# Two B blocks of column pair 1 kept in DRAM in 16 bits, and a new last pair for the row groups of a matmul in Strassen-Winograd form

## The chip, the cores and the metric

The kernel runs on one core of a Trainium2 chip. The metric is the device time of one execution in microseconds (us); a time "before" is the median of three runs of the kernel without the change. The engines are TensorE (PE; weight loads are listed apart as PEld), VectorE (DVE), ScalarE (ACT), GpSimd (POOL) and SyncE (SP). SP, ACT and POOL also issue DMAs, each through a queue of its own, and each issues in program order.

## The reference

```python
# a, b: float32, 4096 x 4096; alpha = 0.01
x = np.matmul(a, b)
return np.where(x > 0, x, alpha * x)
```

The output is float32. The kernel multiplies in 16 bits. It also measures the operands while it runs (row sums of squares of A, sums of squares of B) and has a branch at the end that does the work again in another 16-bit format where the measures ask for it; with this input the branch isn't taken.

## The kernel before, in words

**Tiles.** The output is cut into 4 row groups of 1024 rows (index g) and 4 column pairs of 1024 columns (index j). One (g, j) is a *region*. In a region, A's 1024 rows and B's 1024 columns are each halved in both directions: a11, a12, a21, a22 (512 rows by 2048 of the contraction) and b11, b12, b21, b22 (2048 by 512 columns). Each block is held as two units of 1024 in the contraction (k = 0, 1); a unit is 1 MB in 16 bits. Region (0, 0) is computed plainly while the first data arrive (lines 286 to 483). All others use seven block products instead of eight (line 636), in the order a11, a12, s2, s3, s1, a22, s4, where s1 to s4 are sums of A blocks and B's partners are sums too. They are made on VectorE, A's by `sum_a` (549, the work at 541) once for a row group, B's by `b_sum` (569, 571) in place in every region. In the regions of groups 1 to 3 that don't turn (see below; the code's `in_quarters`), products 5 and 6, and product 3 too except in a group's first region, are cut into quarter products (735).

**A region's course** (the loop from 766). A product (785) sums 64 matmuls into four banks, y or z, by turns. Product 0 goes to y, which ScalarE copies out (`keep`, 798); product 1 to z, which VectorE adds to it (`add`, 942); VectorE applies the leaky function (309) and SP stores the result (948). Product 2 goes on top of y and ScalarE copies y again; product 3 opens z, copied by ScalarE; product 4 goes on top of y, and VectorE adds y to product 3's copy; product 5 goes on top of z, which VectorE adds; product 6 goes on top of y, and ScalarE copies it. So a product that goes on top of banks waits for the copy or addition that reads them.

**Order of the regions** (490). Group 0: pairs 1, 2, 3. Groups 1 and 3: pairs 2, 0, 1, 3. Group 2: 2, 0, 3, 1. A group's last region is *turning* (771): beside its own products it brings in the next group's A, except in group 3. A comes in 16 pieces (`pieces_a`, four each for a11, a12, a21, a22): POOL fetches a piece in four DMAs that turn float32 into 16 bits (131) into one of three a16 buffers, VectorE transposes it (140), and ScalarE squares and sums its rows (590). A buffer is free for the next piece when both are done. `bring_a` (973) does the three steps in this order; `fetch_a` and `square_a` do one. `note_rows` (592, 596) adds the row sums to the measure.

**B's way in.** `fetch_unit` (504) brings one unit of the next region's B. Pair 2 (`CACHED`) is written to DRAM in 16 bits in group 0 and comes back from there by SP (512). All other units come from the float32 input by POOL, two DMAs each, which turn them into 16 bits on the way (515). `fetch_b` is called four times in a region: for b12 after product 3, for b11 after product 4, for b21 before product 6, for b22 after it. The tiles of a block have two buffers, so a fetch waits until the present region's unit has been used for the last time.

**B's measure.** `Measure` (214) squares a block's four parts on ScalarE (229) and sums and folds them on VectorE (238 to 262). `EARLY` (627) lists the blocks measured at a region's start, `MEASURED` (630) those at other places, `IN_ROOM` (634) the block measured in a turning region, in the room of the tile that the next group's s2 will take. Each block of each pair is measured once.

**Nothing is scheduled by a tool.** Every engine does its instructions in the order of the code. What a line comes after in the code, on its engine, is what it waits behind. The lines that the change touches are 490 (order), 504 to 519 (`fetch_unit`), 627 to 634 (where blocks are measured), 1036 to 1071 (between products 1 and 3) and 1091 to 1132 (between product 3 and product 5).

Of the kernel before, what the change touches and what calls it, by code (L numbers as in the profile page):

```python
# [8 lines left out]
P = 128  # L9
DT = mybir.dt.float16  # L10
# [14 lines left out]
KC = 8  # L25
# [5 lines left out]
NT = 512  # L31
MT = 4
RM = MT * P

TURNS = [[0], [0, 1], [1, 2, 3], [2, 3]]
CACHED = 2

# [7 lines left out]
def kernel(  # L47
# [17 lines left out]
    nc = tc.nc  # L65
# [4 lines left out]
    G = M // (2 * RM)  # L70
# [8 lines left out]
    dram_pool = ctx.enter_context(tc.tile_pool(name="kept", bufs=1, space=bass.MemoryType.DRAM))  # L79
# [16 lines left out]
    half = per * P // 2  # L96
# [77 lines left out]
    def rows_of(mat, u, c, wide, whole):  # L174

        if u >= 2 or whole:
            per = 2 * KC
            k0 = u // 2 * 2 * KW
            c += u % 2 * KC
        else:  # L180
            per = KC // RUNS[u]
            k0 = u * KW + c // per * per * P
        return mat[k0:k0 + per * P, :].rearrange("(p c) n -> p c n", p=P)[:, c % per:c % per + wide, :]
# [153 lines left out]
    for what, i, *more in order:  # L337
        if what == "a":
            r, tiles = more
            k = slice(r * rw, (r + 1) * rw)  # L340
# [106 lines left out]
    for i in range(1, len(steps)):  # L447
        t, h, u, first, last = steps[i]
# [16 lines left out]
        t, h, u, first, last = steps[i]  # L465
# [20 lines left out]
    kept = dram_pool.tile([2, KU * KW, NT], DT, name="kept")  # L486

    kept_t = {name: dram_pool.tile([2, P, KC * NT], DT, name=f"kept_{name}") for name in ("t3", "t2")}
    regions = [(0, j) for j in range(1, J)]
    regions += [(g, j) for g in range(1, G) for j in ([2, 0, 3, 1] if g == 2 else [2, 0, 1, 3])]  # L490

    def fetch_b(i, quads, ks):

# [10 lines left out]
    def fetch_unit(i, u, nt):  # L504
        g, j = regions[i]
        half = u // 2
        t = b_pool.tile([P, KC, NT], DT, name="b", tag=f"b{half + 1}{nt + 1}")
        have_b[i, u, nt] = t
        if g > 1 and j == CACHED and (half, nt) == (0, 1):
            move_t("t3", t, u, False)  # L510
        elif g and j == CACHED:
            nc.sync.dma_start(t, rows_of(kept[nt], u, 0, KC, True))
        else:
            for c in range(0, KC, 4):
                nc.gpsimd.dma_start(t[:, c:c + 4, :], b_rows(j, u, c, 4, nt, g > 0))  # L515
            if j == CACHED:
                wide = KC // (RUNS + [1, 1])[u]
                for c in range(0, KC, wide):
                    nc.sync.dma_start(rows_of(kept[nt], u, c, wide, False), t[:, c:c + wide, :])
# [29 lines left out]
    def sum_a(g, name):  # L549
        blk = lambda h, half, k: at[g, h, 2 * half + k]  # L550
        if name != "s3" and (g, name, 0) not in s:
            new_s(g, name)
        for k in range(2):
            if name == "s1":
                a_sum(s[g, "s1", k], blk(1, 0, k), blk(1, 1, k), ADD)
            elif name == "s2":
                a_sum(s[g, "s2", k], s[g, "s1", k], blk(0, 0, k), SUB)
            elif name == "s3":
                s[g, "s3", k] = blk(1, 0, k)
                a_sum(s[g, "s3", k], blk(0, 0, k), blk(1, 0, k), SUB)  # L560
            else:
                a_sum(s[g, "s4", k], blk(0, 1, k), s[g, "s2", k], SUB)
# [29 lines left out]
    def note_rows(but=0):  # L592
        while len(rows_made) > but:
            r = rows_made.pop(0)
            for n, op in enumerate((MAX, MIN, ADD)):
                nc.vector.tensor_tensor(stats[:, n, 0], stats[:, n, 0], r, op)

    def judge(line):
# [26 lines left out]
    A11, A12, A22 = (0, 0, 0), (0, 0, 1), (0, 1, 1)  # L625
    B11, B12, B21, B22 = ((1, half, nt) for half in range(2) for nt in range(2))
    EARLY = {
        (1, 0): [B11], (1, 1): [B11, B21], (2, 0): [B12, B21], (2, 3): [B11], (3, 1): [B12], (3, 3): [B21],
    }
    MEASURED = {  # L630
        (0, 1): (None, [A11], B12, B11), (0, 2): (B21, [B22, A22], B12, A12),
        (3, 0): (B22, [], None, None),
    }
    IN_ROOM = {(1, 3): B22, (2, 1): B22}

    PRODUCTS = [("a11", 0, 0), ("a12", 1, 0), ("s2", 0, 0), ("s3", 0, 1), ("s1", 0, 0), ("a22", 1, 0), ("s4", 1, 1)]

# [14 lines left out]
    def b_quarter(t):  # L652
        return t.rearrange("p (c n) -> p c n", n=HALF)

    def quarters_of_b(i, half, nt):
        return {(k, n): have_b[i, 2 * half + k, nt][:, :, n * HALF:(n + 1) * HALF]
                for k in range(2) for n in range(2)}
# [8 lines left out]
    def sums_of_b(y, to, some=(2, 4, 1)):  # L666
        tt = nc.vector.tensor_tensor
        f = lambda n: b_quarter(to[n])
        if 2 in some:
            tt(f(2), y[0, 1], y[0, 0], ADD)  # L670
        if 4 in some:
            tt(f(4), y[1, 0], f(2), SUB)
        if 1 in some:
            tt(f(1), y[1, 1], f(2), SUB)  # L674
# [27 lines left out]
    def load_x21(g, name):  # L702

        if g:
            for c in range(KC // 2):
                nc.sync.dma_start(by_chunk(x21(g, name))[:, c], by_chunk(kept_x21[name])[:, c])

    def sums_of_s3(g, some, room=None):

        x = {key: by_chunk(q) for key, q in quarters_of_a(g, "s3").items()}  # L710
        rooms = s3_rooms(g)
        sx = {n: by_chunk(room) for n, room in rooms.items()}
        for n in some:
            if n == 4:
                sx[4] = by_chunk(room)
            x0, x1, op = {1: (x[1, 0], x[1, 1], ADD), 2: (sx[1], x[0, 0], SUB),
                          3: (x[0, 0], x[1, 0], SUB), 4: (x[0, 1], sx[2], SUB)}[n]
            nc.vector.tensor_tensor(sx[n], x0, x1, op)  # L718
            if n == 4:
                nc.sync.dma_start(kept_s3, room)  # L720
# [45 lines left out]
    for i, (g, j) in enumerate(regions):  # L766

        ks = (1, 0) if in_quarters else (0, 1)
# [3 lines left out]
        B = lambda half, nt, k: have_b[i, 2 * half + k, nt]  # L772
# [184 lines left out]
        coming = {}  # L957
# [5 lines left out]
        def fetch_a(h, half, n):  # L963
            if n == 0:
                coming["rows", h, half] = small_pool.tile([P, 16], FP32, name="rows", tag=f"rows{half}")
            coming[h, half][n][0]()

        def square_a(h, half, n):
            square_rows(coming[h, half][n][1].held[0], n, coming["rows", h, half])
            if n == MT - 1:  # L970
                rows_made.append(coming["rows", h, half])

        def bring_a(h, half, some=range(MT)):
            if turning:
                for n in some:
                    fetch_a(h, half, n)
                    coming[h, half][n][1]()
                    square_a(h, half, n)
# [19 lines left out]
        for n, m in enumerate(early):  # L998
            if n:
                m.begin()  # L1000
            m.end()
        have_t2 = g > 1 and j == CACHED
        if have_t2:
            for k in ks:
                t = have_b[i, k, 0] = b_pool.tile([P, KC, NT], DT, name="b", tag="b11")
# [4 lines left out]
        for k in ks:  # L1010
# [5 lines left out]
            b_sum(B(0, 0, k), B(0, 1, k), B(0, 0, k), ADD)  # L1016
            if g == 1 and j == CACHED:
                move_t("t3", B(0, 1, k), k, True)
# [17 lines left out]
        if in_fourth:  # L1036
            tq = {n: new_a16() for n in (2, 4)}
            sx4 = new_a16()
            if not second_of_group:
                nc.sync.dma_start(sx4, kept_s3)  # L1040
            t3_of_b(quarters_of_b(i, 0, 1))
            sums_of_b(quarters_of_b(i, 0, 1), tq, (2, 4))
            if second_of_group:
                sums_of_s3(g, (4,), sx4)
        for k in ks:
            b_sum(B(1, 0, k), B(1, 0, k), B(0, 0, k), SUB)
        if first_of_group and g:
# [10 lines left out]
        if in_quarters:  # L1058
            t = x_pool.tile([P, 4, QUARTER], DT, name="q", tag="x")
# [3 lines left out]
        for k in ks:  # L1063
            b_sum(B(0, 0, k), B(1, 1, k), B(0, 0, k), SUB)
        if g:
            bring_a(0, 1)
        note_rows(1)
        if i == 0:
            sum_a(g, "s4")
        if late_ones:  # L1070
            late_ones[0].end()
        if in_quarters and first_of_group:
# [14 lines left out]
        if in_quarters:  # L1087
            tq = {2: t[:, 0], 1: t[:, 1], 4: t[:, 2]}
        fetch_b(i + 1, [(0, 1)], (1, 0) if in_fourth else ks)
        in_room = None  # L1090
        if turning:
            room = new_s(g + 1, "s2").rearrange("p k c m e -> p (k c m e)").bitcast(BF16)
            if (g, j) in IN_ROOM:
                in_room = measure(i, *IN_ROOM[g, j], room.rearrange("p (n w) -> p n w", n=4))
                in_room.begin()
            bring_a(1, 0, [0])
            if in_room:
                in_room.end()
            bring_a(1, 0, [1])
            for n in (2, 3):  # L1100
                fetch_a(1, 0, n)
            load_x21(g, "a22")
            load_x21(g, "s4")
        for m in late_ones[1:]:
# [18 lines left out]
        if in_quarters:  # L1123
            tq, sq = sixth_in_quarters(u2_pairs, [new_bank(zbank + mt) for mt in range(MT)], v_pairs, v, y, tq, sq)
# [1 line left out]
            add(v, y)  # L1126
            leave(v_pairs, 1, 1)
        if turning:
            for n in (2, 3):
                coming[1, 0][n][1]()  # L1130
                square_a(1, 0, n)
            note_rows(1)
# [48 lines left out]
    with inputs.Else():  # L1181
        for m in range(M // RM):
            a_blocks = []
            for u in range(KU):
                t = a_pool.tile([P, KC // 2, RM, 2], BF16, name="a", tag=f"a{u // 2 + 1}{m % 2 + 1}")
# [6 lines left out]
            for n in range(N // NT):  # L1192
                banks = [new_bank(n % 2 * 4 + mt) for mt in range(MT)]
                cols = slice(n * NT, (n + 1) * NT)
                for u in range(KU):
                    t = b_pool.tile([P, KC, NT], BF16, name="b", tag=f"b{u // 2 + 1}{n % 2 + 1}")
# [8 lines left out]
                for mt in range(MT):  # L1205
                    t = c_pool.tile([P, 2, NT], FP32, name="c", tag=f"c{side}")[:, 0]
# [38 lines left out]
```

## Time and profile before

| what | before |
|---|---|
| runs | 1562.06, 1563.91, 1565.93 us; median 1563.91 |
| profiled execution, its own time | 1564.15 us |
| its span, first to last instruction | 1562.4 us |
| mean granted TensorE clock | 0.995 |
| busy: VectorE, ScalarE, POOL | 1138.7, 424.3, 300.4 us |
| TensorE's waits, whole list | 16.1 us |
| DMA | 339.71 MB, mean 217 GB/s |

Some regions in the same execution:

| region | from, to (us) | length | VectorE busy | ScalarE busy | DMA share |
|---|---|---|---|---|---|
| (0,1) | 122.56 to 219.26 | 96.70 | 77.17 | 28.66 | 0.89 |
| (0,3), turning | 315.95 to 412.64 | 96.69 | 61.67 | 49.03 | 0.97 |
| (1,2), after a turn | 412.64 to 506.16 | 93.52 | 84.43 | 13.91 | 0.92 |
| (1,3), turning | 690.03 to 794.77 | 104.74 | 68.20 | 51.57 | 0.95 |
| (2,2), after a turn | 794.77 to 890.28 | 95.51 | 78.24 | 17.84 | 0.96 |
| (2,1), turning | 1074.26 to 1180.96 | 106.70 | 68.21 | 51.57 | 0.94 |

How to read the views: a row of the timeline gives start and length in us, engine, line, operation, tiles, shapes and count, and in square brackets how long the engine stood idle before it and what ended that. A row of the waits gives who waited for whom, the total in us, how often, and the longest. A row of windows gives the stretch, its length, the busy time of PE, PEld, DVE, ACT and POOL with their counts, the granted clock of TensorE (1.00 is full speed), the DMA share and GB/s. A row of the queues gives packets, MB, and the time of the packets as a share of 16 DMA engines' span. An idle engine matters only where TensorE waits for it.

### The profile page before, as it was taken

Reading aid. Unit: us, or ns where it says so; the run is one execution under the profiler, and the core shown is the slowest. Engines: PE = TensorE matmul, PEld = TensorE weight load, DVE = VectorE, ACT = ScalarE, POOL = GpSimd, SP = SyncE. Lnnn points to the kernel's source line nnn. Section 1 sums busy time; section 2 is a strip of 40 time slices with the busy share of each in tenths; the row PEclk is TensorE's granted clock in tenths of the full one; section 3 lists DMA queues with packets and bytes.
Section 4 is the critical chain, followed back from the end, with each engine's and each line's share of the span. In section 5 each row is a group of like instructions: output and inputs, shape, how many; then the busy total and the mean of one; then the engine's idle time right before and its main releaser. Section 6 shows DMA issues by size and latency. Waiting matters only on the chain. (4 is left out here: it accounts for less than half of the span.)

```text
span 1562.4 us, 21610 instructions
## 1 busy us (share of the span) xinstructions
PE 1535.1 (98%) x8571; PEld 838.1 (54%) x8571; DVE 1138.7 (73%) x1179; ACT 424.3 (27%) x730; POOL 300.4 (19%) x482
## 2 busy tenths in 40 slices
PE   9999999999999999999899999999989999999997
PEld 4444444444447475574344757566434475746656
DVE  4378758766697787857569897674956967777686
ACT  2201224646300214105631130211553103021310
POOL 5641110243102020123310202012331110201100
PEclk9999999999999999999999999999999999999999
DMA  9999794998889899699698969979979895998933
GB/s 246 185 216 188 153 280 145 186 186 183 244 311 284 197 207 250 170 270 224 140 283 274 294 167 253 220 171 277 212 150 296 239 281 141 260 221 163 272 119 138
DMA packets 217729, 339.71 MB, mean 217 GB/s; under 512 B 19089, under 2 KB 162705, under 8 KB 209682
## 3 DMA queue, kind: packets, MB, share of 16 engines
q0 software_dynamic: 149376, 141.59, 56.7%
q1 hardware_dynamic: 61618, 171.08, 30.2%
q10 hardware_dynamic: 6624, 25.56, 4.3%
q8 instruction: 69, 1.13, 0.3%
q14 instruction: 42, 0.34, 0.1%
HBM read 374.34 MB, written 103.29 MB: 306 GB/s over the span
## 5 line engine op out<-in xcount | busy, mean ns | idle before, releaser
L785 PE MATMUL ps<-b,a 128*128 128x512 f16 x2752 | 600.8, 379 | 6.3 <-ACT c L798 4.6
L785 PE MATMUL ps<-b,s 128*128 128x512 f16 x2240 | 494.3, 381 | 7.4 <-DVE c L942 7.3
L785 PEld LDWEIGHTS <-a 128*128 128x128 f16 x2752 | 269.0, 98 | 332.1 <-issue 10.4
L785 PEld LDWEIGHTS <-s 128*128 128x128 f16 x2240 | 220.1, 98 | 274.9 <-issue 15.3
L515 POOL DMA_DIRECT2D b<-in_b_dram x184 | 136.6, 747 | 902.5 <-PE ps L735 348.1
L571 DVE TENSOR_TENSOR b<-b 128x4096 f16<-128x4096 f16 x104 | 235.1, 2288 | 80.9 <-DMA b<-in_b_dram 71.6
L798 ACT COPY c<-ps 128x512 f32<-128x512 f32 x172 | 88.6, 596 | 448.2 <-PE ps L785 397.5
L140 DVE STREAM_TRANSPOSE a<-a 128x512 uint32<-128x512 uint32 (+2 forms) x120 | 127.0, 1105 | 106.5 <-DMA a<-in_a_dram 106.5
L131 POOL DMA_DIRECT2D a<-in_a_dram x252 | 137.8, 552 | 234.9 <-ACT junk L590 82.7
L590 ACT ACTIVATE junk<-a 128x512 bf16<-128x512 f16 x192 | 121.1, 631 | 138.4 <-DMA a<-in_a_dram 113.4
L735 PEld LDWEIGHTS <-q 128*128 128x128 f16 x1392 | 136.1, 98 | 16.3 <-DVE q L718 0.6
L309 DVE SCALAR_TENSOR_TENSOR c<-c 128x1024 f32<-128x1024 f32 (+1 forms) x121 | 141.4, 1209 | 4.4 <-ACT c L798 4.2
L942 DVE TENSOR_TENSOR c<-ps,c 128x512 f32<-128x512 f32 x142 | 88.8, 683 | 49.2 <-PE ps L785 32.7
L229 ACT ACTIVATE sq<-b 128x2048 bf16<-128x2048 f16 x56 | 104.4, 1910 | 59.9 <-DVE sq L238 42.4
L281 PE MATMUL ps<-b,a 128*128 128x512 f16 x512 | 112.7, 379 | 2.0 <-DMA b<-in_b_dram 0.9
L735 PEld LDWEIGHTS <-a 128*128 128x128 f16 x1040 | 101.7, 98 | 15.8 <-DVE q L674 0.4
L735 PE MATMUL ps<-b,q 128*128 128x256 f16 x752 | 88.1, 273 | 0.3 <-DVE q L718 0.3
L281 PEld LDWEIGHTS <-a 128*128 128x128 f16 x512 | 49.7, 98 | 62.8 <-issue 3.9
L883 ACT COPY c<-ps 128x512 f32<-128x512 f32 x9 | 5.3, 586 | 268.7 <-PE ps L735 179.0
L735 PE MATMUL ps<-b,a 128*128 128x256 f16 x656 | 77.2, 273 | 0.0
L836 DVE TENSOR_TENSOR c<-ps,c 128x512 f32<-128x512 f32 x80 | 52.3, 685 | 14.8 <-PE ps L735 14.8
L735 PEld LDWEIGHTS <-s 128*128 128x128 f16 x592 | 57.9, 98 | 6.7
(112 smaller groups left out, 880.5 us busy)
## 6 DMA issues: line engine op xcount, KB each, us to landing
b<-in_b_dram POOLq DMA_DIRECT2D x192, 512.0 KB, 15.0
out_dram<-c SPq DMA_DIRECT2D x240, 256.0 KB, 6.1
a<-in_a_dram POOLq DMA_DIRECT2D x244, 128.0 KB, 5.7
b<-kept SPq DMA_DIRECT2D x20, 1024.0 KB, 9.9
q<-kept_qs ACTq DMA_DIRECT2D x40, 512.0 KB, 7.8
s<-kept_s SPq DMA_DIRECT2D x18, 1024.0 KB, 7.3
q<-kept_qa SPq DMA_DIRECT2D x28, 512.0 KB, 7.3
b<-in_b_dram POOLq DMA_DIRECT2D x24, 256.0 KB, 9.1
```

Of the source, the lines that this page charges most:

```text
L131: nc.gpsimd.dma_start(a16[32 * q:32 * q + 32], src.rearrange("(g i) w -> i g w", i=32))
L140: nc.vector.transpose(part.rearrange("p c m e -> p c (m e)").bitcast(U32) .rearrange("p c (g i) -> p g c i", i=32), src[:, :, i * n:(i + 1 ...
L229: nc.scalar.activation(to, self.parts[n], SQUARE)
L281: nc.tensor.matmul(ps, a_cols(at[0, h, u], c, mt, (h, u) == (0, 0)), bt[0, u, nt][:, c, :], start=first, stop=last,)
L309: nc.vector.scalar_tensor_tensor(t, t, alpha, t, op0=MULT, op1=MAX if alpha <= 1 else MIN)
L515: nc.gpsimd.dma_start(t[:, c:c + 4, :], b_rows(j, u, c, 4, nt, g > 0))
L571: nc.vector.tensor_tensor(f(to), f(x0), f(x1), op)
L590: nc.scalar.activation(junk, piece[:, q, :], SQUARE, accum_out=to[:, 4 * n + q:4 * n + q + 1])
L735: nc.tensor.matmul(to[m], xq[:, c // 2, rows, c % 2], yq[:, c, :], start=first and c == 0 and m < banks, stop=c == KC - 1, skip_group_chec ...
L785: nc.tensor.matmul(banks[mt], a_cols(t, c, mt, t is first_a), B(half, nt, k)[:, c, :], start=first and (k, c) == todo[0], stop=(k, c) == t ...
L798: nc.scalar.copy(kept[mt], banks[mt])
L942: nc.vector.tensor_add(to, bank, to)
```

## The change

`kept_last` is a new DRAM tensor. In region (0,1) the four units of b21 and b22 are stored there by SP in 16 bits, after product 1's outputs, before b21 is overwritten by its sum; groups 1 to 3 load these units of pair 1 from there by SP, and no longer from the input by POOL. s4's sum of group 0 moves ahead of b21's sums in (0,1). The order of groups 1 and 2 becomes 2, 0, 3, 1, so that regions (0,3), (1,1) and (2,1) turn. b22's measure in a turning region is now made in (0,3) and (1,1), directly after product 3's copies and at one go; (2,1) has none of this kind. `EARLY` is rearranged to match. In a turn of groups 1 and 2, a12's last piece comes after product 3's copies and that measure; in every turn, of a21's pieces only the first is transposed and squared ahead of product 4's addition, and the other three after it (before: two and two). s3's fourth sum of a group's second region in quarters moves between two B sums.

Counted in the built program: TensorE has the same instructions in the same order; SP gains 4 stores and 12 loads; POOL loses 24 loads of half a unit; VectorE and ScalarE have as many instructions as before.

```diff
 CACHED = 2
+LAST = 1
...
     kept_t = {name: dram_pool.tile([2, P, KC * NT], DT, name=f"kept_{name}") for name in ("t3", "t2")}
+    kept_last = dram_pool.tile([2, 2, P, KC * NT], DT, name="kept_last")
     regions = [(0, j) for j in range(1, J)]
-    regions += [(g, j) for g in range(1, G) for j in ([2, 0, 3, 1] if g == 2 else [2, 0, 1, 3])]
+    regions += [(g, j) for g in range(1, G) for j in ([2, 0, 3, 1] if g < G - 1 else [2, 0, 1, 3])]
...
             nc.sync.dma_start(t, rows_of(kept[nt], u, 0, KC, True))
+        elif g and j == LAST and half:
+            nc.sync.dma_start(t.rearrange("p c n -> p (c n)"), kept_last[u - 2, nt])
         else:
...
     EARLY = {
-        (1, 0): [B11], (1, 1): [B11, B21], (2, 0): [B12, B21], (2, 3): [B11], (3, 1): [B12], (3, 3): [B21],
+        (1, 0): [B11], (1, 3): [B11], (2, 0): [B12, B21], (2, 3): [B21], (2, 1): [B12], (3, 1): [B11, B21],
     }
...
-    IN_ROOM = {(1, 3): B22, (2, 1): B22}
+    IN_ROOM = {(0, 3): B22, (1, 1): B22}
...
-            sums_of_b(quarters_of_b(i, 0, 1), tq, (2, 4))
+            sums_of_b(quarters_of_b(i, 0, 1), tq, (2,))
             if second_of_group:
                 sums_of_s3(g, (4,), sx4)
+            sums_of_b(quarters_of_b(i, 0, 1), tq, (4,))
+        if (g, j) == (0, LAST):
+            for nt in range(2):
+                for k in ks:
+                    nc.sync.dma_start(kept_last[k, nt], B(1, nt, k).rearrange("p c n -> p (c n)"))
+        if i == 0:
+            sum_a(g, "s4")
         for k in ks:
             b_sum(B(1, 0, k), B(1, 0, k), B(0, 0, k), SUB)
...
         if g:
-            bring_a(0, 1)
-        note_rows(1)
-        if i == 0:
-            sum_a(g, "s4")
+            bring_a(0, 1, range(3))
...
                 in_room.begin()
-            bring_a(1, 0, [0])
-            if in_room:
                 in_room.end()
-            bring_a(1, 0, [1])
-            for n in (2, 3):
+            if g:
+                bring_a(0, 1, [3])
+            note_rows(1)
+            for n in range(3):
                 fetch_a(1, 0, n)
+            coming[1, 0][0][1]()
+            square_a(1, 0, 0)
+            fetch_a(1, 0, 3)
             load_x21(g, "a22")
             load_x21(g, "s4")
...
         if turning:
-            for n in (2, 3):
+            for n in range(1, MT):
                 coming[1, 0][n][1]()
                 square_a(1, 0, n)
             note_rows(1)
```

## The prediction

> **What bounds the kernel now.** The reading starts with the page's busy shares, then asks the list of waits what TensorE waits for, then the timeline where those waits lie. A region (g, j) is row group g with column pair j; its seven products are counted 0 to 6, each of 64 matmuls, and the 16 pieces of A that a turning region brings in are counted 1 to 16 (a11: 1 to 4, a12: 5 to 8, a21: 9 to 12, a22: 13 to 16).
>
> ```profile
> PE 1535.1 (98%) x8571; PEld 838.1 (54%) x8571; DVE 1138.7 (73%) x1179; ACT 424.3 (27%) x730; POOL 300.4 (19%) x482
> ```
>
> ```profile
> PE ps L785 <- DVE c L942: 7.3, 5, 3.3
> PE ps L785 <- ACT c L798: 4.6, 4, 2.2
> ```
>
> TensorE is the bound, and the change leaves its instructions in the same order. All that can be won is its waiting: 16.1 us in the whole list, 11.9 of it in these two rows, and what a wait costs after it. The timeline puts both rows into regions (1,3) and (2,1) and the product after them: the two that bring in the rows of the next group in the middle of the kernel. TensorE in (1,3), then in the next region from 794.77:
>
> ```profile
> 731.47 13.98 PE L785 MATMUL ps<-b,a 128*128 128x512 f16 x64
> 745.28 13.98 PE L785 MATMUL ps<-b,s 128*128 128x512 f16 x64
> 759.76 14.79 PE L785 MATMUL ps<-b,a 128*128 128x512 f16 x64 [0.50 <-ACT c L798]
> 777.89 17.02 PE L785 MATMUL ps<-b,s 128*128 128x512 f16 x64 [3.34 <-DVE c L942]
> 794.77 13.99 PE L785 MATMUL ps<-b,a 128*128 128x512 f16 x64
> 809.76 14.79 PE L785 MATMUL ps<-b,a 128*128 128x512 f16 x64 [1.00 <-ACT c L798]
> ```
>
> An undisturbed product takes 13.81 us from start to start. From 690.03 (product 0) to 824.39 (product 2 of the next region) are nine products, 124.32 us; they took 134.36, so this turn loses **10.04 us**. In (2,1) and after, from 1074.26 to 1210.50, it is 136.24, a loss of **11.92 us**. Region (0,3), which turns too, loses nothing (96.69 us for seven).
>
> The cause stands in the other engines' timelines of (1,3), ScalarE first, then VectorE:
>
> ```profile
> 756.26 0.63 ACT L590 ACTIVATE junk<-a 128x512 bf16<-128x512 f16 x1 [11.14 <-DMA a<-in_a_dram]
> ...
> 759.15 2.03 ACT L798 COPY c<-ps 128x512 f32<-128x512 f32 x4
> 761.05 5.54 ACT L229 ACTIVATE s<-b 128x2048 bf16<-128x2048 f16 x3
> ```
>
> ```profile
> 760.37 2.10 DVE L140 STREAM_TRANSPOSE a<-a 128x512 uint32<-128x512 uint32 x2 [1.76 <-DMA a<-in_a_dram]
> ...
> 771.29 1.23 DVE L241 TENSOR_TENSOR s<-s 128x2048 bf16<-128x2048 bf16 x1 [3.45 <-ACT s L229]
> ...
> 775.19 2.07 DVE L140 STREAM_TRANSPOSE a<-a 128x512 uint32<-128x512 uint32 x2
> 777.19 2.44 DVE L942 TENSOR_TENSOR c<-ps,c 128x512 f32<-128x512 f32 x4
> ```
>
> ScalarE has product 3's copies (L798) queued behind the squares of piece 8, which waited 11.14 us for its data, so the copies begin at 759.15 instead of 745.3. B22's measure follows them and is late by as much; VectorE, in order, does the measure and piece 10 before it reads product 4's banks (L942) at 777.19, although product 4 ended at 759.1. Product 6 needs those banks and waits 3.34 us.
>
> **What a wait costs.** Product 6 took 3.04 us more than its 13.98 after the wait: its first four matmuls follow the four additions, and the clock falls:
>
> ```profile
> 770.00:780.00 10.00, 6.62 (x26) 2.38 (x24) 8.54 (x15) 9.65 (x25) 4.05 (x8) 0.84 0.42 61
> 780.00:790.00 10.00, 10.00 (x39) 4.21 (x38) 10.00 (x15) 3.06 (x10) 4.30 (x8) 0.82 1.05 300
> ```
>
> Third column from the right is the granted clock: 0.84 and 0.82, against 1.00 in all other stretches I read. After the waits of 0.50 and 1.00 us the clock stays 1.00, and the 0.81 us extra is the spacing of the copies. [...]
>
> **The change, part by part.**
>
> *Order in turns 1 and 2, now (1,1) and (2,1).* Piece 8 goes behind product 3's copies. In (1,1), with (1,3)'s times (both are entered by a region in quarters): piece 7's squares end at 745.1, copies 745.3 to 747.3, three squares of B22 (5.54) to 752.9, the fourth (1.89) to 754.8; VectorE's sums and folding (1.23 + 0.69 + 0.42 + 0.45 + 0.69 + 0.35 after the last square) end at 758.6. Piece 8, landed at 756.3, is transposed to 760.7, piece 9, landed at 760.4, to 763.1 with the small L596; L942 then runs 763.1 to 765.5. Product 6 now starts at 6 x 13.81 after 690.03, 772.9: **7.4 us to spare**. Later pieces: 10, 11 and 12 are transposed behind L942, to about 775; 14 and 15, released by 11 and 12, are fetched at about 772 and 775 instead of 784.5. They took 18.7 us to land beside the next region's B11 and B21; with as many again they land by 794, and product 6's copies, due before 800.5, follow their squares at 797. (2,1) has no measure there any more (B12's is at its start, where product 0 covers 7.4 us of squares and VectorE was idle 12.30 us), so L942 waits for product 4 only. Both losses go: -10.04 and -11.92.
>
> *B21 and B22 of pair 1 from DRAM.* Twelve loads of 1 MB leave POOL (24 issues of 0.75 us) for SP. By the queue table:
>
> ```profile
> q0 software_dynamic: 149376, 141.59, 56.7%
> q1 hardware_dynamic: 61618, 171.08, 30.2%
> ```
>
> POOL's queue costs 0.567 x 1562.4 / 141.59 = 6.3 us of all 16 DMA engines per MB landed, SP's 2.8: 14 us less for each of three regions. In (1,3), B22's last load was issued at 690.49 and VectorE waited for it until 713.27, POOL holding back piece 1's parts behind it; now it lands near 698 (loads of 1 MB take 7.3 to 9.9) and pieces 1 to 3 come some 8 us sooner. That widens the margins above; TensorE gains nothing itself. On SP, B21's pair stands ahead of four stores of c and B22's ahead of s2's load; those wait for TensorE at 675 to 690.5 as POOL did, s2 (7.3) lands by about 701 and is due at 717.7. Hidden.
>
> *Storing them in (0,1).* Four stores of 1 MB stand on SP behind product 1's outputs (issued 159.08 to 161.05). DMA share there is 0.01 (150 to 160) and 0.27 (160 to 170). s4's two sums (4.49) move ahead of B21's, which must wait for its stores; queued behind are B11's second sums, due for product 4 at 177.82, A11's folding and, behind its last square, product 3's copies (due 191.6). The trace shows no such store. Bounds: kept tiles land in 3.9 to 18.0 us, the kept_t ones, four in a row, in 5.1 to 11.3. With 7 and 9 (the latter, nearest rows): B21's sums end at 170.6 and 173.1, B11's first at 175.3. At 18.0 it would be 8 us late. I take 0.
>
> *B22's measure in (0,3).* It comes after the copies at 372.9: folded by about 384.5, piece 9 to 386.8, L942 to 389.3 (385.0 before; due 398.8). Pieces 10 to 13 slip; 13 is fetched at 394 instead of 379 and shares the DMA engines with 14, 15 and B11, B21: one more piece, 0.5 MB x 6.3 = 3.2 us, so 15 and 16 come 3 to 5 us later. VectorE then has no gap until this row in (1,2), due before product 3 at 454.08:
>
> ```profile
> 447.79 2.48 DVE L942 TENSOR_TENSOR c<-ps,c 128x512 f32<-128x512 f32 x4
> ```
>
> It ends at 450.27, a slack of 3.8; late by 3 to 5 gives 0 to 1.2. I take 0.6.
>
> *The rest.* s3's fourth sum moves ahead of a B sum: TensorE's wait of 0.32 at L718 goes. EARLY measures change regions, covered by product 0 as (1,1)'s two are now.
>
> **Sum.** The profiled run took 1564.15 (span 1562.4, 1.75 around it), 0.24 above the median 1563.91. 1564.15 - 10.04 - 11.92 - 0.32 + 0.6 = **1542.5 us**.
>
> **Rivals.**
> 1. *VectorE's full stretch gives some back* in (0,1) or (1,2): stores that land after 12 us, pieces 6 us late. Two waits of 2.5 us, and 2 for the clock after one: 1549.5. For it: VectorE is 84.4 of 93.5 us busy in (1,2). Against: the margins above.
> 2. *One turn keeps its loss*, because (1,1) still has B22's measure ahead of L942 and two pieces behind it: pieces 8 and 9 landing 8 us later (14 and 15 took 18.7) is enough: 1542.5 + 10 = 1552.5.
> 3. *Both waits only move*, to product 6's copies behind piece 15's squares: about 1563.
> 4. *Slower.* Pieces 10 to 12 now hold their buffers until after L942. If 12 and then 15 each take 18.7 us in all three turns, 15 is transposed at about 428 in (0,3)'s case, the sums s1, s2 and B11's end at 453 instead of 438.7, product 2 (440.27) and 3 wait some 8 us, with 2 for the clock: 10 a turn, 1541.9 + 30 = 1572. It decides from 9 us a turn, piece 15 landing 13 us later than the 411.5 of (0,3). Against: POOL's lighter queue, and product 5 covers piece 12.
>
> **Chances.** Forecast 0.70, rivals 0.11, 0.08, 0.05, 0.06. A difference under 0.3% (4.7 us) can't be told from none. Faster: 0.70 + 0.11 + 0.08 = 0.89; within: 0.05; slower: 0.06. The range takes in the forecast (runs scatter by 2 us to each side) and the first two rivals: 1540 to 1553.
>
> **What would show it.** Right: L942 and L798 gone from TensorE's waits in (1,1), (2,1) and after; product 3's copies at its end; granted clock 1.00 throughout; about 96.7 us for every turn. Wrong: a wait at product 4 in (0,1) (stores), at product 3 in (1,2) (late pieces), or copies of product 6 behind squares at a region's start.

## The result, and the profile after

The changed kernel takes **1550.8 us** (median of six runs, 1548.89 to 1552.31) against 1562.97 for the kernel before (median of its six runs beside them): a ratio of **0.9919**, 95% interval 0.9906 to 0.9931. It is faster, by 12.2 us; 21.4 had been forecast, and the time lies inside the range. The profiled execution took 1550.65 us, its span is 1548.9 (13.5 less than before).

The page's busy shares, two rows of TensorE's waits and the two DMA queues, all of the kernel after:

```profile
PE 1530.1 (99%) x8571; PEld 838.1 (54%) x8571; DVE 1138.8 (74%) x1179; ACT 425.1 (27%) x730; POOL 282.5 (18%) x458
```

```profile
PE ps L789 <- DVE b L575: 5.8, 1, 5.8
...
PE ps L789 <- DVE c L946: 0.4, 2, 0.2
```

```profile
q0 software_dynamic: 136704, 129.00, 52.4%
q1 hardware_dynamic: 63922, 187.86, 33.0%
```

Lines have moved by four (L942 is now L946, L798 is L802). The additions' row fell from 7.3 to 0.4 us, the row of ScalarE's copies is gone, and a row that did not exist before is at the top: TensorE waits once, for 5.8 us, for a sum of B blocks. POOL's queue moved 12.6 MB less (141.59 before) and SP's 16.8 MB more (171.08).

**The two turns lose nothing now.** TensorE in (1,1), products 4 to 6 and, in one row of 128 matmuls, the next region's products 0 and 1, then ScalarE and VectorE there:

```profile
754.96 13.98 PE L789 MATMUL ps<-b,s 128*128 128x512 f16 x64
768.77 13.98 PE L789 MATMUL ps<-b,a 128*128 128x512 f16 x64
782.58 13.98 PE L789 MATMUL ps<-b,s 128*128 128x512 f16 x64
796.39 27.79 PE L789 MATMUL ps<-b,a 128*128 128x512 f16 x128
```

```profile
754.51 2.05 ACT L802 COPY c<-ps 128x512 f32<-128x512 f32 x4 [2.85 <-PE ps L789]
756.42 7.34 ACT L230 ACTIVATE s<-b 128x2048 bf16<-128x2048 f16 x4
```

```profile
769.93 2.10 DVE L141 STREAM_TRANSPOSE a<-a 128x512 uint32<-128x512 uint32 x2
771.95 2.44 DVE L946 TENSOR_TENSOR c<-ps,c 128x512 f32<-128x512 f32 x4
```

Products start every 13.81 us, without a bracket behind them. The copies (L802) now wait for TensorE and no longer for a piece's squares; B22's measure (L230) runs in one piece behind them; the addition is done at 774.4, and product 6, which needs it, starts at 782.58: 8.2 us to spare, where before it waited 3.34. Nine products from 699.70 take 124.32 us (134.36 before); (2,1) takes 96.70 (106.70 before) and the region after it is undisturbed.

**The loss is in (1,2),** the region after the first turn: 412.87 to 515.84, 102.97 us against 93.52 before. TensorE's products 3 and 4 there, after:

```profile
455.80 13.33 PE L789 MATMUL ps<-b,a 128*128 128x512 f16 x61 [0.22 <-DVE c L946]
474.91 16.63 PE L789 MATMUL ps<-b,s 128*128 128x512 f16 x64 [5.78 <-DVE b L575]
```

VectorE there, first before, then after:

```profile
459.26 1.22 DVE L684 TENSOR_TENSOR q<-s 128x2048 f16<-128x2048 f16 x1
460.89 1.22 DVE L684 TENSOR_TENSOR q<-s,q 128x2048 f16<-128x2048 f16 x1 [0.41 <-DMA kept_qs<-q]
462.03 4.49 DVE L571 TENSOR_TENSOR b<-b 128x4096 f16<-128x4096 f16 x2
```

```profile
464.73 1.22 DVE L688 TENSOR_TENSOR q<-s 128x2048 f16<-128x2048 f16 x1
471.43 1.23 DVE L688 TENSOR_TENSOR q<-s,q 128x2048 f16<-128x2048 f16 x1 [5.48 <-DMA kept_qs<-q]
472.57 4.49 DVE L575 TENSOR_TENSOR b<-b 128x4096 f16<-128x4096 f16 x2
```

VectorE makes four quarter sums of s4 here (L684, now L688) and SP stores each as it is made. They go into the three a16 buffers, so the fourth sum waits until the first has been stored, and B11's sums for product 4 stand behind it. VectorE comes 5.47 us later than before (464.73 against 459.26), and the store's wait grows by another 5.07 (5.48 against 0.41): B11's sums start 10.54 later. Before, the first of them (2.24 us) was done at 464.3 for a product that began at 467.90: 3.6 us of slack. What is left, 10.54 - 3.6 = 6.9, is within 0.1 what product 4 is late by against before (474.91 - 467.90 = 7.0). It then takes 2.65 us more than 13.98. 7.0 + 2.65, less the 0.23 by which the region began later, is 9.4 of the 9.45 that (1,2) lost.

Why the wait grew: in the DMA view of those stretches (issues, KB each, median us from issue to landing) the same four stores, before and then after:

```profile
kept_qs<-q SPq DMA_DIRECT2D x4, 512.0 KB, 4.0
```

```profile
kept_qs<-q SPq DMA_DIRECT2D x4, 512.0 KB, 7.8
```

Before, the first was issued at 458.1 and POOL's loads of the next region's b12, which turn float32 into 16 bits, at 461.45; after, at 463.58 and 462.52. So the first store, which the fourth sum waits for, used to land (by 460.89) ahead of the loads and now runs beside them.

In (0,1), where the new stores stand, TensorE waits for nothing. The 13.5 us between the two spans are made up so: turns -21.96, L718 -0.32, (1,2) +9.45, and -0.7 of small shifts, which is what is left over.

### The profile page after: what moved, and what is told of

Read it like the earlier page. It is cut to its first block, busy times and chain, and to the rows that moved or that the text cites. A ratio compares the mean times of both kernels' runs of the same rounds, so it can differ in the third digit from the quotient of the medians.

```text
span 1548.9 us, 21600 instructions
## 1 busy us (share of the span) xinstructions
PE 1530.1 (99%) x8571; PEld 838.1 (54%) x8571; DVE 1138.8 (74%) x1179; ACT 425.1 (27%) x730; POOL 282.5 (18%) x458
## 4 chain that ended last, share of the span: by engine, by line
PE 69%; DVE 3%; DMA 2%; ACT 1%; issue 1%; POOL 0%; DVEq 0%; ACTq 0%
PE ps L789 47%; PE ps L739 21%; DMA a<-in_a_dram 1%; DVE b L575 1%; DVE s L545 1%; DMA kept_qs<-q 0%; ACT junk L594 0%; ACT s L230 0%; DVE c L310 0%; DVE a L545 0%; DVE a L141 0%; DVE c L946 0%; DVE q L688 0%; POOL a L132 0%; DVE c L937 0%
## 5 line engine op out<-in xcount | busy, mean ns | idle before, releaser
L519 POOL DMA_DIRECT2D b<-in_b_dram x160 | 118.8, 747 | 876.9 <-PE ps L739 316.8
L802 ACT COPY c<-ps 128x512 f32<-128x512 f32 x172 | 88.8, 595 | 477.0 <-PE ps L789 407.0
L946 DVE TENSOR_TENSOR c<-ps,c 128x512 f32<-128x512 f32 x142 | 88.8, 682 | 59.7 <-PE ps L789 46.3
L230 ACT ACTIVATE sq<-b 128x2048 bf16<-128x2048 f16 x56 | 104.3, 1910 | 55.2 <-DVE sq L239 40.7
```

The costliest lines, as they stand in the source:

```text
L230: nc.scalar.activation(to, self.parts[n], SQUARE)
L802: nc.scalar.copy(kept[mt], banks[mt])
L946: nc.vector.tensor_add(to, bank, to)
```

## The experiments

Ratios are to the kernel before, run beside each one on the same chip, with the 95% interval. Two questions: what costs the 9.45 us in (1,2), and which part of the change frees the turns.

### What costs time in (1,2)

**No measure in (0,3).** Pair 3's b22 isn't measured at all: its part of B's sum of squares is left out.

```diff
-    IN_ROOM = {(0, 3): B22, (1, 1): B22}
+    IN_ROOM = {(1, 1): B22}
```

> Leaves out the measure of b22 of pair 3 (no IN_ROOM in region (0,3)); everything else as in the changed kernel. Theory M (the measure in (0,3) delays the A pieces, VectorE enters (1,2) 5 us late, a store of s4's quarter sums then meets b12's loads, and product 4 of (1,2) waits 5.78 us and runs with a lower clock): the loss of 9.4 us in (1,2) goes, 1541.5 us. Rival O (the order of a21's pieces does it: the second piece is transposed behind L946 and so piece 13 is fetched at 392 instead of 379, with or without the measure): the loss stays in good part, 1547 to 1551, with product 4's wait in (1,2) still there.

Measured: 1541.18 us, **0.9859** (0.9843 to 0.9876). TensorE waits for nothing in (1,2), and the fourth sum there is back to its old wait:

```profile
460.70 1.22 DVE L688 TENSOR_TENSOR q<-s,q 128x2048 f16<-128x2048 f16 x1 [0.36 <-DMA kept_qs<-q]
```

So the measure's new place costs it, and not the order of the pieces, which this kernel has too.

**The measure in another place.** The same, with b22 of pair 3 measured in (3,3), the kernel's last region; all is computed.

```diff
-        (3, 0): (B22, [], None, None),
+        (3, 0): (B22, [], None, None), (3, 3): (B22, [], None, None),
...
-    IN_ROOM = {(0, 3): B22, (1, 1): B22}
+    IN_ROOM = {(1, 1): B22}
```

> The changed kernel with b22 of pair 3 measured in (3,3), after product 0's copies, instead of in (0,3); the new order of a21's pieces stays in (0,3). Nothing is left out. Theory M (the measure in (0,3) alone costs what (1,2) lost): 1541.5 us, no wait in (1,2), (1,1), (2,1). Rival: (3,3) does not cover the measure, a TensorE wait of 1 to 5 us there: 1543 to 1547.

Measured: 1542.66 us, **0.987** (0.9852 to 0.9888); no waits but those of the start. It computes all that the reference and the measure ask for, and is faster than the kernel after.

**The same with the old order of pieces in (0,3).** The four a21 pieces are brought in there as before the change.

```diff
+        (3, 0): (B22, [], None, None), (3, 3): (B22, [], None, None),
...
+    IN_ROOM = {(1, 1): B22}
...
+            else:
+                bring_a(1, 0, [0, 1])
+                for n in (2, 3):
+                    fetch_a(1, 0, n)
...
-            for n in range(1, MT):
+            for n in range(1 if g else 2, MT):
```

> b22 of pair 3 is measured in (3,3), after product 0's copies as (3,0)'s is, and not in (0,3); region (0,3) has its former order (two of a21's pieces ahead of product 4's addition). Nothing is left out. Both theories M and O expect (0,3) and (1,2) to be as in the kernel before (no loss there) and the turns (1,1) and (2,1) as in the changed kernel: 1541.5 us, if (3,3) covers the measure. If the squares of b22 in (3,3) hold ScalarE or VectorE past what product 2 or 3 needs, it is 1 to 5 us more, with a TensorE wait in (3,3).

Measured: 1541.92 us, **0.9861** (0.9844 to 0.9879), not told apart from the one above. In (0,3) the order of the pieces is worth nothing either way.

**s4's quarter sums behind B11's sums,** so that their wait no longer holds up product 4:

```diff
             keep_x21(g, "s4")
-            sums_of_a(g, "s4", new_a16)
...
             b_sum(B(0, 0, k), B(1, 1, k), B(0, 0, k), SUB)
+        if first_of_group and g:
+            sums_of_a(g, "s4", new_a16)
```

> In a group's first region, s4's four quarter sums (L688) move behind B11's second sums (L575), which product 4 needs; nothing is left out. If the wait of VectorE's fourth quarter sum for a store (5.48 us) is what makes product 4 wait, the 5.78 us and the slow clock behind them (2.7) go though VectorE still enters (1,2) 5 us late: 1542 to 1543 us, with waits of at most 0.5 at product 3 and perhaps 1 later on. Rival (VectorE simply has too much to do in (1,2)): the wait comes back at product 5 and the time stays at 1549 to 1551 us.

Measured: 1552.56 us, **0.9937** (0.9918 to 0.9957): no gain. Product 4 is on time (468.67), but the sums wait for stores three times (4.21, 0.82 and 4.09 us), and product 5's quarter sum (L678) stands behind them:

```profile
489.55 3.59 PE L739 MATMUL ps<-q,q 128*128 128x256 f16 x16 [5.15 <-DVE q L678]
```

The wait moves to the next product that VectorE feeds: product 4 was only the first to be hit, and I had expected the loss to go.

**b12's loads later.** In a group's first region they are issued behind b11's, after product 4, so that they don't meet the stores.

```diff
-        fetch_b(i + 1, [(0, 1)], (1, 0) if in_fourth else ks)
+        b12_later = first_of_group and g > 0
+        if not b12_later:
+            fetch_b(i + 1, [(0, 1)], (1, 0) if in_fourth else ks)
...
         fetch_b(i + 1, [(0, 0)], ks)
+        if b12_later:
+            fetch_b(i + 1, [(0, 1)], ks)
```

> The changed kernel, with the next region's b12 loads moved behind b11's on POOL in the groups' first regions; the measure stays in (0,3), and nothing is left out. If the stores of s4's quarter sums are late (7.8 us to land instead of 4.0) because they meet b12's loads on the DMA engines, the fourth quarter sum's wait in (1,2) falls from 5.48 us to under 1.5, product 4's wait from 5.78 to about 1, with the clock at 1.00: 1543 us. If the stores are late for another reason, or VectorE's work alone is too much, the wait stays at 4 us or more and the time at 1549 to 1552.

Measured: 1567.7 us, **1.0033** (1.0019 to 1.0046), a miss as a whole: b12 now comes too late for the next regions (1,0), (2,0) and (3,0), with new waits of 3.85, 4.30 and 3.42 us for B sums. But in (1,2) itself it answers the question: VectorE is as late as after the change (fourth sum ready for its buffer at 466.6, after at 466.0), and yet its wait is 1.01 us instead of 5.48, product 4 waits 1.31 instead of 5.78, and (1,2) takes 96.65 us, 3.1 more than before the change instead of 9.45. The fourth sum there:

```profile
467.60 1.22 DVE L688 TENSOR_TENSOR q<-s,q 128x2048 f16<-128x2048 f16 x1 [1.01 <-DMA kept_qs<-q]
```

All the kernels that make these sums at the same place (not the one with s4's sums moved), from their timelines in (1,2): how long after product 0 the first s4 sum starts, and how long the fourth then waits for the store (us):

| kernel | first sum after product 0 | fourth's wait |
|---|---|---|
| before; without the turns' measures; with the copy alone | 44.2; 43.0; 43.5 | 0.41; 0.40; 0.35 |
| no measure in (0,3); measure in (3,3); the same, old order in (0,3) | 44.7; 44.6; 42.7 | 0.36; 0.36; 0.36 |
| before, new order of pieces alone | 45.5 | 0.99 |
| measure in (3,3), no copy | 46.7 | 1.05 |
| after, no copy; after, old order of pieces | 48.2; 48.2 | 3.20; 3.80 |
| after; order of regions alone | 49.5; 51.0 | 5.48; 5.31 |
| b12's loads later | 50.3 | 1.01 |

Up to 45 us the wait stays near 0.4; from there to 49.5, 4.8 us more of lateness bring 5.1 us more of waiting: over that range a late us counts about twice, and in the one kernel past it the wait is no longer. The last row, as late but without the loads beside it, shows what it hangs on.

### What frees the turns

**After the change, old order of pieces.** In the turns piece 8 goes back ahead of product 3's copies, and two a21 pieces come ahead of the addition, the measure's sums between them; this holds for (0,3) too, but for piece 8.

```diff
-            bring_a(0, 1, range(3))
+            bring_a(0, 1)
+        note_rows(1)
...
                 in_room.begin()
+            bring_a(1, 0, [0])
+            if in_room:
                 in_room.end()
-            if g:
-                bring_a(0, 1, [3])
...
+            bring_a(1, 0, [1])
...
```

> The changed kernel with the former order inside the turning regions (a12's last piece ahead of product 3's copies, the measure between a21's first two pieces, two of them ahead of product 4's addition); the copy in DRAM, the order of the pairs and the places of the measures stay. Theory (piece 8 ahead of product 3's copies is what made them late): (1,1) loses 4 to 10 us again, (2,1), which has no measure now, 0 to 3, and (1,2) keeps 4 to 9: 1552 to 1562 us. Rival (loads from DRAM and the new order of the pairs free the turns by themselves): no wait in (1,1) and (2,1), 1546 to 1551.

Measured: 1546.6 us, **0.9898** (0.9871 to 0.9924). I had expected one or both turns to lose again; neither does. Product 3's copies are 5 us late (756.4), but product 6 still starts on its beat, with 2.0 us of slack; what remains is (1,2)'s wait (3.72 us). So the order of the pieces is not needed here.

**After the change, loads from the input.** `kept_last`, its stores and its loads go; POOL loads as before.

```diff
-    kept_last = dram_pool.tile([2, 2, P, KC * NT], DT, name="kept_last")
...
-        elif g and j == LAST and half:
-            nc.sync.dma_start(t.rearrange("p c n -> p (c n)"), kept_last[u - 2, nt])
...
-        if (g, j) == (0, LAST):
-            for nt in range(2):
-                for k in ks:
-                    nc.sync.dma_start(kept_last[k, nt], B(1, nt, k).rearrange("p c n -> p (c n)"))
```

> Undoes the DRAM copy alone: b21 and b22 of pair 1 come from the float32 input by POOL again and nothing is stored in (0,1); orders and measures as in the changed kernel. Theory (the new order of the pieces frees the turns; the copy only widens margins, and product 6 of (1,1) has 8 us to spare): 1550.8 us, within 1 us of the changed kernel, no TensorE wait in (1,1) and (2,1), while A's first pieces land some 8 us later there. Rival (the copy is needed): a21's and a22's pieces come late again, L946 or the copies of product 6 are waited for, and 3 to 10 us a turn come back: 1554 to 1570 us.

Measured: 1549.51 us, **0.9917** (0.9893 to 0.994), the same as with the copy. No wait in either turn; product 1 of the region after the first of them waits 0.35 us for late copies, and the nine products lose 1.3 us there. What the copy does is seen in B22's sum in (1,1), which waits for its block: here, and in the kernel of the old order with the copy:

```profile
712.72 2.29 DVE L572 TENSOR_TENSOR b<-b 128x4096 f16<-128x4096 f16 x1 [11.99 <-DMA b<-in_b_dram]
```

```profile
704.63 2.29 DVE L575 TENSOR_TENSOR b<-b 128x4096 f16<-128x4096 f16 x1 [2.44 <-DMA b<-kept_last]
```

With product 0 at 694.57 and 696.02, that is 18.2 and 8.6 us into the region. The copy brings B22's sum, and with it what VectorE does behind it, forward by 9.5 us, and with the new order of pieces nobody is waiting for it.

**The best version without the copy** (measure in (3,3), both edits together):

```diff
-        (3, 0): (B22, [], None, None),
+        (3, 0): (B22, [], None, None), (3, 3): (B22, [], None, None),
...
-    IN_ROOM = {(0, 3): B22, (1, 1): B22}
+    IN_ROOM = {(1, 1): B22}
...
-        elif g and j == LAST and half:
-            nc.sync.dma_start(t.rearrange("p c n -> p (c n)"), kept_last[u - 2, nt])
```

> As the run with the measure in (3,3), and without the DRAM copy: b21 and b22 of pair 1 come from the input by POOL and nothing is stored in (0,1). Theory (the copy widens margins only): 1541.5 us, as with the copy. Rival (the copy carries part of the gain, hidden so far by the loss in (1,2)): 1544 us or more, with a TensorE wait in or after (1,1) or (2,1).

Measured: 1542.62 us, **0.987** (0.9851 to 0.9888), the same as with the copy.

**Neither of the two:** the old order of pieces and loads from the input (both edits above); order of regions and places of the measures as after the change.

```diff
-        elif g and j == LAST and half:
-            nc.sync.dma_start(t.rearrange("p c n -> p (c n)"), kept_last[u - 2, nt])
...
-            bring_a(0, 1, range(3))
+            bring_a(0, 1)
```

> The changed kernel with b21 and b22 of pair 1 from the float32 input and with the old order of pieces in the turns: of the change only the order of the regions and the places of the measures stay. Theory that the old order needs the copy's head start (B22 in (1,1) about 10 us earlier): without it, piece 8 holds product 3's copies back in (1,1) as it did in (1,3) before, and B22's measure VectorE's addition; (1,1) loses about 9 again, (2,1), which has no measure, 0 to 3, and (1,2) keeps the 5 to 9 of the measure in (0,3): 1555 to 1558. Rival, the order of the regions and the places of the measures free the turns by themselves, the copy and the order of pieces are worth nothing each: no wait in (1,1) and (2,1), about 1547.

Measured: 1559.39 us, **0.9974** (0.9961 to 0.9987). Now (1,1) loses again, by the old chain; ScalarE, then TensorE:

```profile
767.14 0.63 ACT L591 ACTIVATE junk<-a 128x512 bf16<-128x512 f16 x1 [11.22 <-DMA a<-in_a_dram]
...
770.04 2.03 ACT L799 COPY c<-ps 128x512 f32<-128x512 f32 x4
```

```profile
788.79 0.38 PE L786 MATMUL ps<-b,s 128*128 128x512 f16 x1 [3.35 <-DVE c L943]
```

Piece 8's squares wait 11.22 us, the copies stand behind them, product 6 waits 3.35. Nine products from 700.87 take 133.20 us, a loss of 8.88; in (2,1), without a measure, 128.20, a loss of 3.88. With one of the two remedies, in the two kernels above that undo one of them each, the first turn loses 0.5 and 1.3 us and the second nothing. The profiled execution of this kernel took 1565.2 us, the longest of its ten and 5.8 above their median, so a typical execution loses less than these rows show.

The next three start from the kernel before. **Without the measures in the turns** (the sums of squares of two b22 blocks are left out):

```diff
-    IN_ROOM = {(1, 3): B22, (2, 1): B22}
+    IN_ROOM = {}
```

> The kernel before, without b22's measures in (1,3) and (2,1) (the sums of squares of b22 of two pairs are left out). Theory that the measure between product 3's copies and the addition is what the turns pay for, and the late copies only a little: TensorE's wait for the addition goes in both turns (3.34 us and its like, with the clock's cost), the copies behind piece 8's squares stay late (waits of about 0.5 to 2.2): 1563 less 22 and 3 to 7 back, 1544 to 1549. Rival, the late pieces are the cause, the measure only fills the time in which VectorE waits for them: 1556 to 1563.

Measured: 1546.72 us, **0.9892** (0.9874 to 0.991). The waits for the addition are gone; product 5 still waits 0.85 and 1.17 us for late copies. The nine products lose 1.8 and 2.2 us instead of 10.04 and 11.92: the measure between copies and addition made 18 of the 22 us.

**With the new order of pieces alone:**

```diff
         if g:
-            bring_a(0, 1)
+            bring_a(0, 1, range(3))
...
                 in_room.begin()
-            bring_a(1, 0, [0])
-            if in_room:
                 in_room.end()
-            bring_a(1, 0, [1])
+            if g:
+                bring_a(0, 1, [3])
+                note_rows(1)
...
-            for n in (2, 3):
+            for n in range(1, MT):
                 coming[1, 0][n][1]()
```

> The kernel before with the new order of pieces in the turns alone: in (1,3) and (2,1) piece 8 behind product 3's copies and B22's measure, in all turns one piece of a21 ahead of product 4's addition and three behind it; old order of regions, loads from the input, measures where they were. Theory of the prediction, the order of the pieces frees both turns: no wait in (1,3), (2,1) and the products after them, about 1542. Rival, the order alone is not enough while B22 comes from the input 10 us later and both turns have its measure: one or both turns lose 5 to 10: 1548 to 1560.

Measured: 1543.69 us, **0.9874** (0.985 to 0.9898). Products 6 and 0 around the end of (1,3), where 3.34 us were waited before:

```profile
773.20 13.98 PE L785 MATMUL ps<-b,s 128*128 128x512 f16 x64
787.01 13.98 PE L785 MATMUL ps<-b,a 128*128 128x512 f16 x64
```

Both turns are free with their measures in place, B from the input and the old order of the regions; 2.4 us are left around product 1 after them. This small part of the change by itself beats the whole.

**With the copy alone** (and s4's sum of group 0 where the change puts it):

```diff
+        elif g and j == LAST and half:
+            nc.sync.dma_start(t.rearrange("p c n -> p (c n)"), kept_last[u - 2, nt])
...
+        if (g, j) == (0, LAST):
+            for nt in range(2):
+                for k in ks:
+                    nc.sync.dma_start(kept_last[k, nt], B(1, nt, k).rearrange("p c n -> p (c n)"))
+        if i == 0:
+            sum_a(g, "s4")
```

> The kernel before with the copy of pair 1's b21 and b22 in DRAM alone (and s4's sum of group 0 ahead of b21's sums, so that the stores have time); regions, measures and order of pieces as before, so only (2,1) turns on a block from the copy, (1,3) on input. Theory that the copy's head start frees a turn with the old order by itself: (2,1) with its measure loses nothing, (1,3) its 10 as before, (1,2) nothing, as no measure stands in (0,3): 1551 to 1553. Rival, the copy helped only together with the new order of the regions: both turns keep their losses, 1560 to 1564.

Measured: 1552.82 us, **0.9942** (0.9922 to 0.9962). Product 6 in (1,3), which turns on pair 3 and so on input, and in (2,1), which turns on the copy:

```profile
778.09 15.85 PE L789 MATMUL ps<-b,s 128*128 128x512 f16 x64 [3.34 <-DVE c L946]
```

```profile
1157.16 13.98 PE L789 MATMUL ps<-b,s 128*128 128x512 f16 x64
```

(2,1) is free with the old order of pieces and its measure in place; (1,3) keeps its loss.

## Why the prediction was right and where it was wrong

- **-10.04 and -11.92 for the turns: right,** to 0.1 us, and by the chain given. The addition in (1,1) was to have 7.4 us to spare and has 8.2. The new order of pieces does it by itself, as the prediction said: the kernel before with that order alone has lost both waits.
- **"That widens the margins above; TensorE gains nothing itself" (the copy): right in this change, incomplete as a reason.** Taking the copy away costs nothing, but only because the new order is there; alone it frees a turn too. It is a second remedy for the same wait, and its gain can't be added to the first one's.
- **Stores in (0,1) at 0: right.** B21's two sums start at 167.14 and 169.69, after waits of 1.21 and 0.25 us for the stores, and B11's sums end at 176.4 for a product 4 at 178.04.
- **-0.32 at L718: right;** the row is gone.
- **B22's measure in (0,3), +0.6: wrong; it measured +9.45.** The first half of the step held: the measure folded at 384.2 (384.5 forecast), the addition at 386.46 (386.8), piece 13 fetched at 393.74 (394). Piece 13 then took 18.8 us to land beside B11 and B21, and the rest was 5.5 us late instead of 3 to 5. What failed is the price. The prediction checked that lateness against one deadline, the addition before product 3, where it cost about what was forecast: product 3 ended 0.84 us late (0.6 forecast). It did not follow VectorE to the next wait behind it: the fourth quarter sum, the store it needs, and the loads of b12 that this store now meets. 5.07 us of extra waiting came from there, and 2.65 of slower matmuls after; the lateness of 5.5 itself, beyond product 4's slack of 3.6, is most of the rest. Against the forecast of 1542.5 this term alone is 8.85 us; with -0.7 of small shifts it gives the profiled 1550.65. The row with 0.41 us of waiting for `kept_qs` stood in the trace of before and would have led there. (The 385.0 given for this addition in (0,3) before the change is not its end, as the 389.3 beside it is: it ran from 384.63 to 387.12. No term of the sum hangs on it.)
- **Rivals.** The first, VectorE's full stretch gives some back (1549.5, chance 0.11), is what happened, and not the forecast of 1542.5 (chance 0.70): it came in (1,2) and by pieces 6 us late, with one wait of 5.78 in place of two of 2.5. Neither turn kept its loss, no wait moved to product 6's copies, and nothing made the kernel slower: the other three fell. The time lies in the range because the range was drawn to take in this rival; the forecast itself is 8.3 us below the measured median.

Every run fits this account: a turn that has the new order or the copy loses at most 1.6 us, one with neither 9 to 12 if it has a measure (2 to 4 if it has none); and a measure in (0,3) costs (1,2) about 5 to 9.5, or 3 where b12's loads come later. How much the late wait in (1,2) slows product 4 can be read from the granted clock (0.50 for 6.83 us, below); what starts a slow stretch is not settled.

## What to carry to other kernels

When an edit makes an in-order engine late, follow it past its first deadline: at each instruction behind it that itself waits (for a buffer, a store, a block), ask whether what it waits for is also made late, and which transfers it will then meet. Where a change has several parts that attack one wait, their gains don't add; measure each part alone before keeping all of them. Here one of them, the order of the pieces, brings the whole gain, and the move of a measure that came with it gave nearly half of it back.

## What the runs showed of the hardware

**Stores beside loads.** Four stores of 512 KB by SP landed in 4.0 us (median) when the first of them was ahead of POOL's converting loads and in 7.8 beside those loads. In the kernel with b12's loads later, where none of these loads was issued before 478.47, the fourth sum waited 1.01 us for the first store, against 5.48 after the change.

**What a wait costs afterwards is not told by its length.** Matmul product after its wait, against its undisturbed time (13.98 us, or 14.79 where ScalarE's copies or VectorE's additions space its start): 5.78 us of waiting +2.65; 5.61 +1.33; 4.30 +2.58; 3.85 +1.68; 3.72 +1.69; 3.42 +1.36; 3.34 +2.23 in (1,3) before and +1.06 in the kernel with the copy alone; 3.03 +1.70; 1.22 +1.69 (product 5 of (2,1) with the order of regions alone); 2.18 +0.00 (product 5 of (2,1) before); 1.31, in the kernel with b12's loads later, +0.01. In the first of these the granted clock, third column from the right, is low in the stretch of the wait and the product's start; three narrower stretches show where:

```profile
470.00:480.00 10.00, 5.09 (x12) 1.79 (x13) 8.54 (x6) 0.57 (x2) 0.91 (x2) 0.67 1.15 283
```

```profile
470.00:473.48 3.48, 0.00 (x0) 0.00 (x0) 2.05 (x2) 0.57 (x2) 0.91 (x2) 1.00 1.11 330
473.48:480.31 6.83, 5.40 (x13) 1.94 (x14) 6.79 (x5) 0.00 (x0) 0.00 (x0) 0.50 1.18 255
480.31:490.00 9.69, 9.69 (x46) 4.41 (x45) 9.54 (x9) 0.00 (x0) 1.48 (x2) 1.00 1.11 339
```

The clock is at half for 6.83 us, from within the wait into product 4. TensorE is busy in 5.40 of them (the first busy column); at half speed half of that, 2.70 us, is lost (an estimate), and 2.65 was measured. The kernel before has two such stretches, one from within the wait of 3.34 before product 6 of (1,3), one from 2.07 us after the start of product 6 of (2,1), which had waited 3.34 too:

```profile
776.76:783.58 6.82, 5.65 (x13) 1.74 (x13) 6.82 (x9) 3.28 (x10) 2.15 (x4) 0.50 0.69 130
1165.87:1169.28 3.41, 3.41 (x10) 1.23 (x9) 3.41 (x4) 0.20 (x2) 0.01 (x1) 0.50 1.11 203
```

The same estimate gives 2.8 and 1.7 us; the first product took 2.23 more than 14.79, the second, in four rows from 1163.80 to 1180.60, 2.01. The additions space the start of both, spacing and slow clock overlap, and the estimate is rougher. With the order of regions alone the granted clock is 0.84 and 0.99 in the two stretches of 10 us from 470 to 490, where the wait of 5.61 ends, and 0.83 from 1150 to 1160, where that of 1.22 does: 1.7 us of clock in each case (an estimate: 10 x 0.16 + 10 x 0.01, and 10 x 0.17), beside products that took 1.33 and 1.69 more. For the waits of 3.03, 3.42, 3.72, 3.85 and 4.30 the product's time is measured, and the clock isn't shown. That the cost is what of the slow stretch falls on the product is therefore shown in the kernel after, and roughly in two others. What starts a slow stretch is not settled: after the wait of 2.18 us the clock stayed at 1.00 (1143.00 to 1160.46, before), after that of 1.31 the product took 13.99 us, and with that of 1.22 there was a slow stretch.
